# A fixed TensorE order for the RWKV preparation: one stretch of small products per pair, head sums in shared banks

## The chip, the cores and the metric

The kernel runs on one core of a Trainium2 chip. The metric is the device time of one execution in microseconds (us). TensorE multiplies matrices out of SBUF into the eight banks of PSUM; VectorE (DVE) and ScalarE (ACT) read those banks and compute elementwise; GpSimd (POOL) works on SBUF alone; transfers are issued from the queues of SyncE (SP), ScalarE and GpSimd. The engines run side by side and wait for each other through semaphores.

## What is computed

One decoder layer on 512 tokens of width 1024, in float32. Attention sub-layer: a norm, one wide input projection, and two mixers on its columns, a sparse attention (compressed, selected and window branches) and an RWKV-7 mixer with 8 heads of 64; both are projected, merged by gates, projected again and added. Channel sub-layer: norm, a gated MLP with a short causal convolution, add. The change lies in the preparation of the RWKV mixer, of which this is the core:

```python
xl = p_in + (shifted - p_in) * mu
r, k, v, xw, xa, xg = jnp.split(xl, RWKV_SPLITS, axis=-1)
w = -jax.nn.softplus(-(w0 + jnp.tanh(xw) @ w2)) - 0.5
decay = jnp.exp(-jnp.exp(w.astype(jnp.float32)))
a = jax.nn.sigmoid(a0 + xa @ a2)
...
kk = k * k_k.reshape(H, N).astype(jnp.float32)
kk = kk / jnp.maximum(jnp.sqrt(jnp.sum(kk * kk, axis=-1, keepdims=True)), 1e-12)
k = k * (1.0 + (a - 1.0) * k_a.reshape(H, N).astype(jnp.float32))
...
y = y + jnp.sum(r * k * r_k, axis=-1, keepdims=True) * v
```

Two sums over the 64 channels of a head stand in it: the norm of `kk` (key sum) and the bonus `sum(r * k * r_k)`.

## The kernel before

Activations lie with channels on the 128 partitions and the 512 tokens along the row; two heads share a tile, so the 8 heads make four pairs p = 0 to 3 (`NH2`). To keep float32 accuracy every large product is made of three: weights and activations are split into a high and a low part (`whi`, `wlo`; `hh`, `hl`), and a dense tile of 128 columns (`dense_fm`, line 414) is 8 steps of `whi` times `hh` and `whi` times `hl`, then 8 of `wlo` times `hh`: 24 products of 128x128 by 512. Each dense tile takes the next weight tile from a fixed list (`weight_tiles`, line 215): `wnext` starts the load of a later tile on SP, splits the one after (`wsplit_`: high part on ScalarE, low part on VectorE or GpSimd, line 296) and hands out the one in turn.

For a pair the preparation has these steps. `front(p)` (492): the dense tile of keys, the two decay products `zw` and `za` (64 rows each, on the two halves of the array), token shift (`shift_mix`: one ScalarE and one VectorE operation out of the bank), tanh, a cumulative sum by a VectorE scan, two exponentials `ep` and `pi`. `norms(p)` (516): squares of the scaled keys (`kk`), the key sum as one product of the block matrix `ones` with `kk`, maximum, logarithm, exponential, giving `rn`. `receptance(p)` and `values_of(p)`: the dense tiles of `rx` and `vx`. `values_tok(p)` (538): four transposes of `vx` into one bank and four ScalarE copies into `UV`. `vectors(p)` (548): some ten VectorE operations from these to `AR`, `bh` and `tv`, then the bonus sum as one product of `ones` with `tv`, times `vx`, into `BO`. `gram(p)` (567): 16 transposes of `bh` into two banks, copied to `BKT` by ScalarE; then 32 products of `bh` with `AR` in two halves of four chunks, each into two banks, masked by VectorE into `AB`.

PSUM banks come from three rings: `mmb()` with four banks, `pa()` and `pb()` with two each. A product that starts a bank waits until the last reader of that bank's previous content is done.

The order of the instructions on each engine is chosen when the program is built, from the order in the text, the dependencies and estimated durations; `tc.high_priority()` moves an instruction ahead. Inside `tc.manual_schedule(engines=...)` the named engines follow the text instead. The preparation is outside such a block before the change, so the small products of one step may stand between the dense products of another.

Behind the preparation, VectorE inverts the 32x32 diagonal blocks of `AB` (lines 617 to 633: four transposes, 62 small operations), transposes the result into `Y1` (730), and `below` (740) multiplies with it on TensorE. In between TensorE makes dense tiles of queries, compressed values and the first key and value windows. The queries' read-out (688 to 692) copies each bank and squares each head into a part of `QK` that serves as scratch. At 696 to 704 the bias table is expanded: a memset on GpSimd, two small loads on ScalarE's queue into the same part of `QK`, one product, one copy, one store.

## Time and profile before

| | us |
|---|---|
| median of 3 runs | 841.3 |
| lowest and highest | 841.02, 841.45 |
| the profiled execution | 841.33 |
| its span in the profile | 839.5 |

The profile is one execution. A row of the list in order of time gives the start from the beginning of the span, the length, the engine, the line, the operation, what it writes and reads, and the shape; several alike are merged into one row with their count, and the idle time of the engine before it, with what ended it, stands in brackets. Almost all operations go through small helpers, so that line 120 is every product, 123 every ScalarE operation, 126 to 135 most of VectorE's: names of tiles tell them apart. A float32 product appears as two instructions, one for each of two passes. Matmuls are pipelined: what counts is the distance from one start to the next, not the length shown. PE is TensorE, ps_mm, ps_a and ps_b are the three rings of banks, kc holds the constants (`ones`, the identity, the mask), prm the parameters.

### The profile page before, as it was taken

How to read it: one execution, taken by the hardware profiler on the slowest of the kernel's cores; microseconds unless marked ns; L12 is line 12 of the kernel's file. 1: busy time of each engine (PE TensorE's matmuls, PEld its weight loads, DVE VectorE, ACT ScalarE, POOL GpSimd, SP SyncE). 2: the span in 40 equal slices, each digit the busy share in tenths (PEclk: the TensorE clock that was granted, in tenths of full speed). 3: DMA queues.
4: the chain of work that ended last, by engine and by line, in shares of the span. 5: the costliest groups of instructions: out<-in, count | busy, mean ns of one | idle time of the engine just before them, and what ended most of it. 6: DMA issues, size and time to landing. Idle time of an engine off the chain costs nothing.

```text
span 839.5 us, 12845 instructions
## 1 busy us (share of the span) xinstructions
PE 824.8 (98%) x5097; PEld 669.9 (80%) x5097; DVE 514.1 (61%) x998; ACT 405.4 (48%) x784; POOL 52.4 (6%) x69
## 2 busy tenths in 40 slices
PE   7999999999999999999999999999999999999998
PEld 6777778887677876777788988888888888888886
DVE  5478779964556678888665566665555666322222
ACT  6766654452555767677343454444444444221210
POOL 5200020140000100111000000000000000000000
PEclk9999999999999999999999999999999999999999
DMA  7432222335462320000266033333333332233421
GB/s 229 113 80 72 76 76 77 83 102 168 128 126 62 84 57 13 26 26 26 63 222 206 1 101 100 94 90 93 101 101 101 100 96 89 92 101 113 138 75 51
DMA packets 109104, 78.73 MB, mean 94 GB/s; under 512 B 3869, under 2 KB 97748, under 8 KB 109044
## 3 DMA queue, kind: packets, MB, share of 16 engines
q1 hardware_dynamic: 106512, 73.51, 29.7%
q10 hardware_dynamic: 1060, 2.55, 1.0%
q0 software_dynamic: 1472, 1.86, 1.0%
q8 instruction: 40, 0.66, 0.3%
q14 instruction: 20, 0.16, 0.1%
HBM read 74.56 MB, written 2.29 MB: 92 GB/s over the span
## 4 chain that ended last, share of the span: by engine, by line
PE 53%; DVE 0%; DVEq 0%; issue 0%
PE ps_mm L120 52%; PE ps_b L203 0%; PE ps_a L203 0%; PE ps_a L120 0%; PE ps_b L1187 0%; PE ps_mm L1187 0%; DVE x L126 0%; DVEq L1379 0%; PE ps_a L1139 0%
## 5 line engine op out<-in xcount | busy, mean ns | idle before, releaser
L296 DVE TENSOR_TENSOR wlo<-raw,whi 128x1024 fp32r<-128x1024 f32 (+1 forms) x111 | 131.5, 1186 | 186.5 <-PE ps_mm L120 157.8
L120 PE MATMUL ps_mm<-hh,whi 128*128 128x512 f32 (+1 forms) x624 | 242.6, 391 | 0.7 <-ACT whi L123 0.7
L120 PE MATMUL ps_mm<-hl,whi 128*128 128x512 f32 (+1 forms) x624 | 240.4, 387 | 0.0
L123 ACT ACTIVATE whi<-raw 128x1024 fp32r<-128x1024 f32 (+3 forms) x124 | 123.3, 996 | 170.9 <-PE ps_mm L120 141.6
L120 PE MATMUL ps_mm<-hh,wlo 128*128 128x512 f32 (+1 forms) x624 | 151.7, 384 | 0.0
L120 PEld LDWEIGHTS ps_mm<-hh,whi 128*128 128x128 f32 x624 | 117.3, 188 | 27.5 <-ACT whi L123 1.1
L120 PEld LDWEIGHTS ps_mm<-hl,whi 128*128 128x128 f32 x624 | 117.4, 188 | 23.4 <-issue 1.0
L120 PEld LDWEIGHTS ps_mm<-hh,wlo 128*128 128x128 f32 x624 | 115.1, 188 | 23.3
L120 PE MATMUL ps_mm<-whi,aT 128*128 128x512 f32 x352 | 84.5, 390 | 0.0
L120 PEld LDWEIGHTS ps_mm<-whi,aT 128*128 128x128 f32 x352 | 65.9, 188 | 14.3 <-issue 0.4
L135 DVE SCALAR_TENSOR_TENSOR cgv<-ps_mm,cw,cgv 128x511 f32<-128x511 f32 (+1 forms) x88 | 65.4, 746 | 1.6
L123 ACT ACTIVATE cgv<-ps_mm,cw 128x512 f32<-128x512 f32 x44 | 34.3, 781 | 23.3 <-PE ps_mm L120 23.3
L120 PE MATMUL ps_mm<-wlo,aT 128*128 128x512 f32 x176 | 44.3, 389 | 0.0
L123 ACT ACTIVATE P<-P,nm 128x512 f32<-128x512 f32 (+3 forms) x64 | 35.4, 553 | 14.9 <-DVE nm L1161 14.9
L123 ACT ACTIVATE aT<-cgv 128x512 fp32r<-128x512 f32 x22 | 13.9, 632 | 56.8 <-DVE cgv L126 56.8
L120 PEld LDWEIGHTS ps_mm<-wlo,aT 128*128 128x128 f32 x176 | 33.0, 188 | 6.9
L123 ACT ACTIVATE cgv<-cgv 128x512 f32<-128x512 f32 x22 | 13.9, 632 | 41.0 <-DVE cgv L135 41.0
L296 POOL TENSOR_TENSOR wlo<-raw,whi 128x512 fp32r<-128x512 f32 (+3 forms) x13 | 20.4, 1569 | 204.3 <-PE ps_mm L120 148.5
L1161 DVE CUSTOM_DVE_ANT_0 P<-ps_a,AB 128x512 f32<-128x512 f32 (+3 forms) x64 | 29.4, 483 | 4.2 <-PE ps_a L120 3.7
L126 DVE TENSOR_TENSOR x<-x,ps_mm 128x512 f32<-128x512 f32 (+1 forms) x17 | 11.0, 654 | 23.0 <-PE ps_mm L120 21.2
L126 DVE TENSOR_TENSOR aT<-cgv,aT 128x512 fp32r<-128x512 f32 x22 | 15.2, 693 | 14.7 <-ACT aT L123 14.7
L120 PE MATMUL ps_a<-KH,qst 128*128 128x512 f32 (+3 forms) x64 | 21.3, 348 | 1.6 <-DVE nm L1161 0.9
(356 smaller groups left out, 1203.4 us busy)
## 6 DMA issues: line engine op xcount, KB each, us to landing
raw<-in_w_up_dram SPq DMA_DIRECT2D x44, 512.0 KB, 3.7
raw<-in_w_in_dram SPq DMA_DIRECT2D x38, 512.0 KB, 3.8
raw<-in_w_down_dram SPq DMA_DIRECT2D x22, 512.0 KB, 3.5
raw<-in_w_out_dram SPq DMA_DIRECT2D x8, 512.0 KB, 3.6
xt<-in_x_dram SPq DMA_DIRECT2D x4, 512.0 KB, 5.9
raw<-in_cmp_w_k_dram SPq DMA_DIRECT2D x4, 512.0 KB, 4.9
raw<-in_cmp_w_v_dram SPq DMA_DIRECT2D x4, 512.0 KB, 5.0
raw<-in_w_proj_b_dram SPq DMA_DIRECT2D x8, 256.0 KB, 2.7
```

Of the source, the lines that this page charges most:

```text
L120: te.matmul(o, lhsT=l, rhs=r, start=start, stop=stop)
L123: sc.activation(o, i, f, **kw)
L126: v.tensor_tensor(o, a, b, op=op)
L135: v.scalar_tensor_tensor(o, a, s, b, op0=op0, op1=op1)
L296: eng.tensor_tensor(lo, raw, hi.bitcast(F32), op=ALU.subtract)
L1161: v.tensor_tensor_reduce(out=P[:, i], in0=sp[:, N * (i - i0):N * (i - i0) + N], in1=BT[:, h, 384 - 128 * qt:512], scale=-1.0, scalar=-NEG, ...
```

## The change

- `front` and the sum in `norms` are taken apart: `keys_of` (dense keys, shift, squares), `decays` (decay products and what follows), `norms` (what follows the sum).
- A head sum is no longer one product of 128x128 by 512. `head_sums` makes four of 64x64 by 256: the first 256 tokens go to bank 0 with the two heads in place, the second 256 to bank 1 with the two heads exchanged, so that the four lie on the four quarters of the array. The readers undo the exchange in pieces (`EXCH`). `sums` puts the key sum of the next pair in columns 0 to 255 and the bonus sum of this pair in columns 256 to 511 of the same two banks.
- `kk` is overwritten with the clipped sum; the maximum is two operations, the last exponential three, the multiplication with `vx` three, each on half or a quarter of the data.
- TensorE's order is written out: vector work of the pair, dense keys and receptance of the next pair, then in one stretch the value transposes, the next pair's decay products, `gram`, the shared sums, and the next pair's dense values. For the last pair but one, decay products lie inside the receptance tile (after 12 of its 24 products) and the key sum right behind it, ahead of the value transposes.
- `gram` takes its transposes' banks and, by pair, one half's banks from `mmb` instead; the copies to `BKT` have priority.
- After the preparation, the squares of the queries are written in place into their bank, and the bias table's memset and two loads come ahead of the queries, the loads on GpSimd's queue.

```diff
--- before.py
+++ after.py
@@ -489,14 +489,18 @@
     L = {}
 
 
-    def front(p):
+    def keys_of(p):
+        kx = t2("kx", 2)
+        shift_mix(dense_fm(hh, hl), 4 + p, kx)
+        kk = t2("kk", 2)
+        act(kk, kx, AF.Square, scale=col("rwkv_k_k", p))
+        L.setdefault(p, {}).update(kx=kx, kk=kk)
+
+    def decays(p):
         cs = slice(128 * p, 128 * p + 128)
-        kx = t2("kx", 2)
-        pk = dense_fm(hh, hl)
         zw, za = pa(), pb()
         mm(zw, wa[0:64, cs], xw[0:64], True, True)
         mm(za, wa[64:128, cs], xw[64:128], True, True)
-        shift_mix(pk, 4 + p, kx)
         cl = t2("cl")
         act(cl, zw, AF.Tanh, scale=0.5, bias=w0h[:, p:p + 1])
         aa = t2("aa", 2)
@@ -511,23 +515,32 @@
         pi = t2("pi", 2)
         act(pi, cum, AF.Exp, scale=-1.0)
         v.tensor_copy(PC[:, p, :, None], ep[:, :, C:C + 1])
-        L[p] = dict(kx=kx, aa=aa, ep=ep, pi=pi)
-
-    def norms(p):
-        kx = L[p]["kx"]
-        kk = t2("kk", 2)
-        act(kk, kx, AF.Square, scale=col("rwkv_k_k", p))
-        ss = pa()
-        mm(ss, ones, kk, True, True)
+        L.setdefault(p, {}).update(aa=aa, ep=ep, pi=pi)
+
+
+
+    def head_sums(src, o, o0=0):
+        for i in range(2):
+            for r in range(2):
+                a, b = slice(64 * r, 64 * r + 64), slice(64 * (r ^ i), 64 * (r ^ i) + 64)
+                mm(o[i][b, o0:o0 + 256], ones[a, a], src[a, 256 * i:256 * i + 256], True, True)
+
+    EXCH = [(slice(0, 128), slice(0, 128), 0), (slice(0, 64), slice(64, 128), 1), (slice(64, 128), slice(0, 64), 1)]
+
+    def norms(p, o):
+        kk = L[p]["kk"]
         rn = t2("rn", 2)
-        ts(rn, ss, 1e-24, None, op0=ALU.max)
-        act(rn, rn, AF.Ln)
-        act(rn, rn, AF.Exp, scale=-0.5)
-        L[p].update(kk=kk, rn=rn)
+        for i in range(2):
+            ts(kk[:, 256 * i:256 * i + 256], o[i][:, 0:256], 1e-24, None, op0=ALU.max)
+        act(kk, kk, AF.Ln)
+        for d, s_, i in EXCH:
+            cs = slice(256 * i, 256 * i + 256)
+            act(rn[d, cs], kk[s_, cs], AF.Exp, scale=-0.5)
+        L[p]["rn"] = rn
 
     def receptance(p):
         rx = t2("rx", 2)
-        shift_mix(dense_fm(hh, hl), p, rx)
+        shift_mix((yield from dense_fm_g(hh, hl)), p, rx)
         L[p]["rx"] = rx
 
     def values_of(p):
@@ -559,23 +572,38 @@
         stt(bh[:, :, 1, :], chunks(kx), 1.0, chunks(pi), ALU.mult, ALU.mult)
         tv = t2("tv")
         stt(tv, rx, col("rwkv_r_k", p), kx, ALU.mult, ALU.mult)
-        L[p]["bh"] = bh
-        bs = pa()
-        mm(bs, ones, tv, True, True)
-        tt(BO[:, p], bs, vx, ALU.mult)
+        L[p].update(bh=bh, tv=tv)
+
+    def bonus(p, o):
+        for d, s_, i in EXCH:
+            cs = slice(256 * i, 256 * i + 256)
+            tt(BO[d, p, cs], o[i][s_, 256:512], L[p]["vx"][d, cs], ALU.mult)
+
+
+    def sums(pk, pb_):
+        o = [pa(), pb()]
+        if pk is not None:
+            head_sums(L[pk]["kk"], o)
+        if pb_ is not None:
+            head_sums(L[pb_]["tv"], o, 256)
+        if pk is not None:
+            norms(pk, o)
+        if pb_ is not None:
+            bonus(pb_, o)
 
     def gram(p):
         bh = L[p]["bh"]
-        ptr = [pb(), pa()]
+        ptr = [mmb(), mmb()]
         for c in range(NCH):
             for r in range(2):
                 rs = slice(64 * r, 64 * r + 64)
                 te.transpose(ptr[r][:, 64 * c:64 * c + 64], bh[rs, c, r:r + 2].rearrange("p a t -> p (a t)"),
                              ident[rs, rs])
-        for r in range(2):
-            act(BKT[:, :, p, r, :], ptr[r].rearrange("p (c j) -> p c j", c=NCH))
+        with tc.high_priority():
+            for r in range(2):
+                act(BKT[:, :, p, r, :], ptr[r].rearrange("p (c j) -> p c j", c=NCH))
         for c0 in range(0, NCH, 4):
-            ptr = [mmb(), mmb()] if c0 else [pb(), pa()]
+            ptr = [mmb(), mmb()] if c0 == (0, 0, 4, -1)[p] else [pb(), pa()]
             for i in range(4):
                 for r in range(2):
                     rs = slice(64 * r, 64 * r + 64)
@@ -586,24 +614,34 @@
                    mask[:, None, :].to_broadcast([128, 4, 128]), ALU.mult)
 
 
-    front(0)
-    norms(0)
-    receptance(0)
-    values_of(0)
-    late_params()
-    for p in range(NH2):
-        if p + 1 < NH2:
-            front(p + 1)
-            norms(p + 1)
-        values_tok(p)
-        vectors(p)
-        if p + 1 < NH2:
-            receptance(p + 1)
-        gram(p)
-        if p + 1 < NH2:
-            values_of(p + 1)
-        if p + 2 == NH2:
-            kcp = dense_fm(hh, hl)
+    with tc.manual_schedule(engines={mybir.EngineType.PE}):
+        keys_of(0)
+        decays(0)
+        run(receptance(0))
+        sums(0, None)
+        values_of(0)
+        late_params()
+        for p in range(NH2):
+            vectors(p)
+            last = p + 2 == NH2
+            if p + 1 < NH2:
+                keys_of(p + 1)
+                rec = receptance(p + 1)
+                next(rec)
+                if last:
+                    decays(p + 1)
+                run(rec)
+                if last:
+                    sums(p + 1, None)
+            values_tok(p)
+            if p + 1 < NH2 and not last:
+                decays(p + 1)
+            gram(p)
+            sums(p + 1 if p + 1 < NH2 and not last else None, p)
+            if p + 1 < NH2:
+                values_of(p + 1)
+            if p + 2 == NH2:
+                kcp = dense_fm(hh, hl)
     dbg("AR", AR)
     dbg("BO", BO)
     close(tp_cm)
@@ -682,21 +720,21 @@
             for r in range(2):
                 act(Dc[64 * r:64 * r + 64, a, g, :], p[64 * g:64 * g + 64, r::2])
 
+    oh, rbx, vb = QK[0:33, 2048:2432], QK[0:33, 2440:2448], QK[0:8, 2560:2944]
+    nc.gpsimd.memset(rbx[32:33], NEG)
+    nc.gpsimd.dma_start(rbx[0:32], A["rel_bias"])
+    nc.gpsimd.dma_start(oh, A["onehot"])
     windows(0, kcp)
     urgent.append(1)
     bq = dense_tok(512, hh, hl)
     for t in range(NT):
         act(qn[:, t], bq[t])
         for h in range(H):
-            act(QK[:, 2048 + 64 * h:2112 + 64 * h], bq[t][:, 64 * h:64 * h + 64], AF.Square,
-                accum_out=qss[:, t, h:h + 1])
+            hs_ = bq[t][:, 64 * h:64 * h + 64]
+            act(hs_, hs_, AF.Square, accum_out=qss[:, t, h:h + 1])
     windows(1, dense_fm(hh, hl))
 
 
-    oh, rbx, vb = QK[0:33, 2048:2432], QK[0:33, 2440:2448], QK[0:8, 2560:2944]
-    nc.gpsimd.memset(rbx[32:33], NEG)
-    sc.dma_start(rbx[0:32], A["rel_bias"])
-    sc.dma_start(oh, A["onehot"])
     pt = pa()
     mm(pt[0:8, 0:384], rbx, oh, True, True)
     act(vb, pt[0:8, 0:384])
```

## The prediction

> **What bounds the kernel now.** I read the page first, then the sums by stretch, then the preparation in order of time on TensorE, and last what ScalarE and VectorE do under it.
>
> ```profile
> span 839.5 us, 12845 instructions
> PE 824.8 (98%) x5097; PEld 669.9 (80%) x5097; DVE 514.1 (61%) x998; ACT 405.4 (48%) x784; POOL 52.4 (6%) x69
> ```
>
> TensorE has 98% of the span and nothing else comes near it. The change touches 31.54 us (first decay product) to 123.03 us (first query product):
>
> ```profile
> 31.54:123.03 91.49, 90.96 (x532) 68.89 (x531) 67.67 (x103) 57.94 (x84) 2.35 (x1) 1.00 0.26 72
> 51.02:73.49 22.47, 22.47 (x133) 17.17 (x133) 17.11 (x27) 14.48 (x21) 0.00 (x0) 1.00 0.18 48
> L120 PE MATMUL ps_mm<-hh,wlo 128*128 128x512 f32 x97 | 24.1, 389 | 0.0
> 29.64 1.98 PE L120 MATMUL ps_mm<-hh,wlo 128*128 128x512 f32 x8
> ```
>
> In the first two rows the numbers after the length are busy time and count of TensorE, its weight loads, VectorE, ScalarE and GpSimd. TensorE is busy 90.96 of 91.49 us at a full granted clock (1.00), VectorE 67.67, ScalarE 57.94, the DMAs 0.26 of their time. The third row counts the low-part products: 97, one begun earlier, so 96, a third of 288 dense products (12 weight tiles of 24). The fourth gives their pitch, (1.98 - 0.389) / 7 = 0.227 us. Dense work is 288 x 0.2265 = 65.2 us, and 91.5 - 65.2 = 26.3 us is everything else on TensorE. In one pair (22.47 us, 72 dense products of 16.3 us) it is 6.2 us. That is what the change can shrink.
>
> **What the small work costs now.** Pair 0 to 1, in order of time, with start and length first:
>
> ```profile
> 50.70 0.39 PE L120 MATMUL ps_mm<-hh,wlo 128*128 128x512 f32 x1
> 51.02 0.69 PE L120 MATMUL ps_a<-xw,wa 64*128 64x512 f32 x1
> 52.08 0.66 PE L542 MATMUL ps_b<-kc,vx 128*128 128x128 f32 x4
> 52.49 0.48 PE L120 MATMUL ps_mm<-hh,whi 128*128 128x512 f32 x1
> 52.81 0.39 PE L120 MATMUL ps_mm<-hl,whi 128*128 128x512 f32 x1
> 54.65 1.02 PE L120 MATMUL ps_a<-kk,kc 128*128 128x512 f32 x2
> 55.52 1.02 PE L120 MATMUL ps_a<-tv,kc 128*128 128x512 f32 x2
> 59.91 0.27 PE L573 MATMUL ps_b<-kc,bh 64*128 64x64 f32 x1
> 60.45 0.33 PE L120 MATMUL ps_b<-AR,bh 64*128 64x128 f32 x1
> 62.39 0.50 PE L120 MATMUL ps_mm<-hh,whi 128*128 128x512 f32 x1
> ```
>
> From start to start: decay pair 51.02 to 52.08, 1.06; value transposes 0.41; a head sum (kk, then tv) 0.87; key transposes 59.91 to 60.45, 0.54; gram products 60.45 to 62.39, 1.94. Leaving a dense run costs 50.70 to 51.02, 0.32 instead of 0.23; returning, 52.49 to 52.81, the same: 0.2 us for a stretch in all. Over four pairs: 4.2 + 1.65 + 7.0 (eight sums) + 2.15 + 7.75, with 0.35 for the parameter transposes, is 23.1. There are 13 stretches (two in the first pair's lead, one for parameters, three for each of three pairs, one at the end): 2.6. The rest, about 0.6 to 0.9, is waiting, most of it at the end:
>
> ```profile
> 118.76 0.66 PE L542 MATMUL ps_b<-kc,vx 128*128 128x128 f32 x4 [0.25 <-DVE vx L135]
> 120.69 0.22 PE L573 MATMUL ps_a<-kc,bh 64*128 64x64 f32 x1
> 121.05 0.37 PE L120 MATMUL ps_b<-AR,bh 64*128 64x128 f32 x1
> 124.18 0.50 PE L120 MATMUL ps_mm<-whi,hh 128*128 128x512 f32 x1 [0.18 <-DVE AB L126]
> ```
>
> **The head sums.** Each becomes four products of 64 rows by 64 columns on four quarters of the array, 256 columns long, two to a bank. No row shows that form at 256. The nearest is the scan:
>
> ```profile
> 187.26 0.27 PE L120 MATMUL ps_b<-Xs,AB 64*64 64x64 f32 x2
> 187.28 0.27 PE L120 MATMUL ps_b<-UV,AB 64*64 64x64 f32 x2
> 187.37 0.23 PE L120 MATMUL ps_b<-Xs,AB 64*64 64x64 f32 x2
> ```
>
> Four quarter products start within 0.02 us and the next four follow 0.1 us later, so quarters run side by side, with the two of one output bank in different partitions. Half the columns of the 0.87 us sum then take 0.43. Bounds: 0.43, or 0.87 if they run in twos. I take 0.43: 8 x 0.44 = 3.5 us gained. [...]
>
> **The order.** Stretches fall from 13 to 8: decay 0, sum 0, parameters, pair 0, pair 1, decay 3, pair 2, pair 3. 5 x 0.2 = 1.0 us gained. Inside a merged stretch the tile shape changes twice; a first product costs 0.33 against 0.27 (60.45 and 59.91 against their followers), about 0.05 each, 0.4 us lost in all. The old waits go (0.9). Sum before new waits: 3.5 + 1.0 - 0.4 + 0.9 = **5.0 us**.
>
> **New waits.** A fixed order cannot slip dense work in while a bank is read out. In pairs 0 and 1 the shared sums need both banks of the decay products, and each of those is released by ScalarE, which in the same stretch has:
>
> ```profile
> L123 ACT ACTIVATE UV<-ps_b 64x256 f32<-64x256 f32 x4 | 1.5, 378 | 0.1
> L123 ACT ACTIVATE cl<-ps_a,w0h 128x512 f32<-128x512 f32 x1 | 0.7, 690 | 0.4 <-PE ps_b L120 0.4
> L123 ACT ACTIVATE rx<-ps_mm,omm 128x512 f32<-128x512 f32 x1 | 0.7, 687 | 0.0
> L123 ACT ACTIVATE aa<-ps_b,a0h 128x512 f32<-128x512 f32 x1 | 0.7, 681 | 0.0
> L123 ACT ACTIVATE BKT<-ps_a 128x512 f32<-128x512 f32 x1 | 0.6, 600 | 0.0
> L123 ACT ACT_TABLE_LOAD x2 | 2.6, 1283 | 0.0
> ```
>
> 1.5 + 0.7 + 0.7 + 0.7 + 2 x 0.6 = 4.8 us, some 4.6 with their overlap. TensorE reaches the sums after 0.41 + 1.06 + 0.54 + 1.94 + 0.1 = 4.05. So about 0.6 us of waiting twice, 1.2; queued behind the sums are only the value products. In pair 2 the bonus sum waits likewise, 0.3 estimated (up to 3, if the logarithm's two table loads of 1.28 go ahead of the transposes' read-out). In pair 3 the second gram half needs the bank of the value transposes; that cost 0.36 before (120.69 to 121.05), and the key copies (2 x 0.6) now have priority over it: 0.6 taken, 0.4 to 1.4 possible. New waits: 1.2 + 0.3 + 0.6 = **2.1 us**, bounds 0 and 5.6.
>
> **What is hidden.** The norm's logarithm and exponential and the bonus come in two and three pieces. A 64-partition, 256-column copy out of PSUM takes 0.43 on VectorE:
>
> ```profile
> L957 DVE COPY UV<-ps_b x8: 427/428/428, 188.9 to 279.7; 64x256 f32<-64x256 f32 x8
> 55.71 0.69 DVE L130 TENSOR_SCALAR rn<-ps_a 128x512 f32<-128x512 f32 x1 [0.19 <-PE ps_a L120]
> 71.21 0.74 DVE L135 SCALAR_TENSOR_TENSOR tv<-rx,prm,kx 128x512 f32<-128x512 f32 x1
> 82.38 0.27 PE L573 MATMUL ps_b<-kc,bh 64*128 64x64 f32 x1
> ```
>
> So three pieces of bonus are 1.3 instead of 0.7 and two of the maximum 0.86 instead of 0.69: +0.8 us of VectorE a pair, 17.9 in some 21.5. The chain from a key sum to the next gram (maximum, logarithm, exponential, eight vector operations) ran from 55.71 to 71.21, 15.5 us, and had until 82.38. Now three dense tiles (16.3) and 1.5 of small work lie between: 17.8. The cover shrinks from 26.7 to 17.8 but holds by 2.3. Price 0; without that cover see the rival below.
>
> After the stage, VectorE runs a long inverse which TensorE meets at `below`:
>
> ```profile
> 124.64 8.16 DVE L625 STREAM_TRANSPOSE inv<-AB 32x1024 f32<-32x1024 f32 x4
> 163.24 4.46 DVE L730 STREAM_TRANSPOSE sg<-inv 32x1024 f32<-32x1024 f32 x2
> 168.94 0.21 PE L120 MATMUL ps_a<-sg,AB 32*32 32x32 f32 x1
> ```
>
> It ends at 167.70, 1.24 us before it is needed. The last bonus (1.3) now stands between masks and transposes, while TensorE has the last sum (0.43 + 0.2) there too: about 0.5 us of slack is left, price 0, bound 0.8.
>
> The moved loads leave ScalarE's queue, where the weight split followed them, for GpSimd's:
>
> ```profile
> 149.14 0.33 ACTq L698 DMA_DIRECT2D QK<-in_rel_bias_dram  x1
> 20.15 0.56 POOL L437 DMA_DIRECT2D wa<-in_rwkv_w_dram  x1 [0.92 <-PE ps_mm L120]
> 124.36 2.40 POOL L296 TENSOR_TENSOR spare<-raw,spare 128x1024 fp32r<-128x1024 f32 x1
> ```
>
> Two issues of 0.33 go from ScalarE; two of 0.56 on GpSimd may delay the spare split, which dense queries use only some 8 us after its end. The squares change only where they write. Price 0, between -0.3 and +0.3.
>
> **Sum.** The profiled execution took 841.33 us, 1.83 around its span of 839.5; the median of the runs, 841.3, is the same. 841.33 - 5.0 + 2.1 = **838.4 us**.
>
> **Rivals.**
> - No new waits: ScalarE keeps ahead as it has 8 of 22.47 us free in a pair. 841.3 - 5.0 = 836.3. Against: its work in the stretch, 4.6, does not fit 4.05.
> - The waits eat the gain, so the merged stretch does not do what it is said to: bounds of 5.6 against 5.0 give 841.9. For: the table loads sit in the same engine. Against: ScalarE is idle elsewhere, so banks can be read before.
> - The quarters do not overlap in one bank: 3.5 lost, 838.4 + 3.5 = 841.9. [...]
> - Slower: the chain to the next gram is late. Its place is VectorE's queue right after the shared sums, where masks (4 x 0.6), bonus (1.3), scale and scan (1.6) now stand ahead of or among the norm: 15.5 + 5.3 = 20.8 against 17.8, 3 us at each of pairs 1, 2 and 3, 838.4 + 9 = 847. It decides from a total of 4.6 us late, since 838.4 + 4.6 = 843.0. Against: in the old 15.5 us four masks and a bonus are already included.
>
> **How the numbers follow.** About 0.2% (1.7 us) is what a measurement of this kernel can tell from no change. Forecast 0.52, no waits 0.16: both faster, 0.68. Waits eat the gain 0.13, quarters 0.05: same, 0.18. Late chain 0.14: slower. The range goes from 835.8 (5.0 gained without a wait, 0.3 from the moved loads, 0.2 more) to 842.5, which holds the two rivals near 841.9 and leaves most of the late chain outside. The forecast's own range is 836.3 to 839.9.
>
> **What would show it.** Right: no kk or tv product of 512 columns; eight stretches; quarter products of a sum starting within 0.02 us, a shared pair of sums in about 0.9 us; a pair's period near 21.4; waits of TensorE on `cl` or `aa` of about 0.6 before the sums. Wrong: a wait on `bh` before the key transposes, a period above 22.5, sums of 1.7 us, or `below` waiting for the inverse.

## The result, and the profile after

The changed kernel takes 844.99 us (median of 6 runs, 844.34 to 845.53) against 841.33 for the kernel before on the same chip: ratio 1.0043, 95% interval 1.0032 to 1.0054. It is 3.7 us slower, where 2.9 us faster was predicted. The page of the profile after:

```profile
span 843.2 us, 12971 instructions
PE 825.1 (98%) x5145; PEld 671.2 (80%) x5145; DVE 516.5 (61%) x1010; ACT 409.2 (49%) x792; POOL 53.3 (6%) x71
```

The span grew by 3.7 us, TensorE's busy time by 0.3. So the time went into TensorE's idle time, except for what a slower clock adds. The sums by stretch, for the preparation and for its pair periods (columns as in the prediction; the granted clock stands behind the five busy times):

```profile
31.45:127.44 95.99, 91.54 (x580) 70.48 (x580) 69.99 (x114) 60.31 (x92) 2.35 (x1) 0.98 0.25 67
55.81:78.05 22.24, 22.24 (x145) 17.62 (x144) 17.06 (x30) 13.42 (x21) 0.00 (x0) 1.00 0.28 71
78.05:103.97 25.92, 23.87 (x149) 17.74 (x148) 18.43 (x30) 15.76 (x25) 0.00 (x0) 1.00 0.25 63
103.97:123.28 19.31, 17.12 (x116) 13.42 (x117) 16.10 (x26) 13.51 (x21) 0.00 (x0) 0.91 0.26 76
...
109.00:112.20 3.20, 3.20 (x31) 2.22 (x27) 2.74 (x5) 3.15 (x6) 0.00 (x0) 0.50 0.42 152
```

The preparation takes 95.99 us, 4.5 more than 91.49. The period of pair 0 to 1, 22.24, is 0.2 shorter than before and has no idle time. In the next one TensorE is idle for 25.92 - 23.87 = 2.05 us, in the third for 2.19, and there its clock falls to half for one stretch of 3.4 us, which costs 1.7. The places, in order of time on TensorE:

```profile
59.98 0.65 PE L120 MATMUL ps_a<-kk,kc 64*64 64x256 f32 x4
60.58 0.43 PE L120 MATMUL ps_b<-kk,kc 64*64 64x256 f32 x2
...
82.47 1.04 PE L120 MATMUL ps_mm<-AR,bh 64*128 64x128 f32 x13 [2.00 <-DVE rx L135]
...
105.12 0.66 PE L555 MATMUL ps_b<-kc,vx 128*128 128x128 f32 x4 [0.49 <-ACT aa L123]
...
108.12 0.37 PE L120 MATMUL ps_b<-AR,bh 64*128 64x128 f32 x1 [1.70 <-DVE kk L130]
...
109.28 1.92 PE L120 MATMUL ps_mm<-AR,bh 64*128 64x128 f32 x16
```

The first two rows show the wait that was predicted: the second bank of the sums is held by `aa`, and its products start at 60.58 instead of within 0.1 of 59.98. It makes the two sums about 0.5 longer: 1.61 here and 1.51 in the next pair, against 1.08 in run 7 below, which does not wait for `aa`. The large waits are others. The gram of pair 1 waits 2.00 for a bank of the ring of four until VectorE has done the shift of `rx`; that of pair 2 waits 1.70 for the bank of the key sum until VectorE has taken its maximum. The last row is the half clock: 16 starts in 1.85 us, where at full clock they take 0.99. Of the 4.5 us lost, 0.9 comes back behind the preparation: `below` starts 4.50 later than before (173.44, 168.94), the last state product of the scan 3.63 later (273.32, 269.69), since in between the kernel before waits 0.69 for the split of a weight that has just landed (212.36) and the changed kernel does not.

Why is VectorE late? ScalarE and VectorE of the kernel after, from one norm to the waiting gram, in order of time:

```profile
64.32 0.42 DVE L130 TENSOR_SCALAR kk<-ps_b 128x256 f32<-128x256 f32 x1
64.82 1.28 ACT L123 ACT_TABLE_LOAD   x1 [2.94 <-DVE kk L130]
...
68.06 1.27 ACT L123 ACTIVATE rn<-kk 128x256 f32<-128x256 f32 x3
69.37 0.75 DVE L135 SCALAR_TENSOR_TENSOR kk<-kx,prm,rn 128x512 f32<-128x512 f32 x1 [3.73 <-ACT rn L123]
...
78.05 0.75 DVE L135 SCALAR_TENSOR_TENSOR kx<-ps_mm,prm,kx 128x511 f32<-128x511 f32 x1
78.83 0.72 ACT L123 ACTIVATE kk<-kx,prm 128x512 f32<-128x512 f32 x1 [5.33 <-DVE kx L135]
81.67 0.74 DVE L135 SCALAR_TENSOR_TENSOR rx<-ps_mm,prm,rx 128x511 f32<-128x511 f32 x1
```

VectorE waits 3.73 us for the exponential `rn`. From 69.37 to 78.05 it is busy without a break (vector work of pair 1, the shift of `vx`, two weight splits), and only then comes the shift of pair 2's `kx`, on which ScalarE has waited for 5.33 us, and behind it, with one split more, that of `rx`. Whatever makes `rn` late makes these shifts late. From this norm to the next one (93.74) neither engine waits for TensorE: VectorE works until 78.80, ScalarE from 78.83 to 83.35 (squares, a weight split, `rx`, `UV`, `cl`), VectorE from 83.38 to 89.12 (scan, masks, maximum, bonus), ScalarE from 89.19 to 93.70 (logarithm, exponentials, two table loads). These 24.37 us are a loop of the two engines alone, and TensorE's waits follow from it. The experiments took that apart.

### The profile page after: what moved, and what is told of

Its sections match the earlier page's. It is cut to its first block, busy times and chain, and to the rows that moved or that the text cites. A ratio compares the mean times of both kernels' runs of the same rounds, so it can differ in the third digit from the quotient of the medians.

```text
span 843.2 us, 12971 instructions
## 1 busy us (share of the span) xinstructions
PE 825.1 (98%) x5145; PEld 671.2 (80%) x5145; DVE 516.5 (61%) x1010; ACT 409.2 (49%) x792; POOL 53.3 (6%) x71
## 4 chain that ended last, share of the span: by engine, by line
PE 53%; DVE 0%; DVEq 0%; issue 0%
PE ps_mm L120 52%; PE ps_a L203 0%; PE ps_b L203 0%; PE ps_a L120 0%; PE ps_b L1225 0%; PE ps_mm L1225 0%; DVE x L126 0%; DVEq L1417 0%; PE ps_a L1177 0%
## 5 line engine op out<-in xcount | busy, mean ns | idle before, releaser
L120 PE MATMUL ps_mm<-whi,hh 128*128 128x280 f32 (+2 forms) x72 | 22.6, 334 | 0.3 <-ACT QK L123 0.3
```

Of the source, the lines that this page charges most:

```text
L120: te.matmul(o, lhsT=l, rhs=r, start=start, stop=stop)
```

## The experiments

Times are medians; each ratio is to the kernel before, run in turn on the same chip. The rows and waits are those of one profiled execution of each. The diffs show the deciding lines, and `...` stands for the others.

**1. The moved loads and squares alone** (the kernel before with these two edits).

```diff
-            act(QK[:, 2048 + 64 * h:2112 + 64 * h], bq[t][:, 64 * h:64 * h + 64], AF.Square,
...
+            act(hs_, hs_, AF.Square, accum_out=qss[:, t, h:h + 1])
...
-    sc.dma_start(rbx[0:32], A["rel_bias"])
+    nc.gpsimd.dma_start(rbx[0:32], A["rel_bias"])
...
```

> The kernel before with only the last part of the change: squares in place, the bias table's two loads ahead of the queries on GpSimd's queue. Theory W (the loss is bank waits of the fixed order: 2.2 us on rx in pair 1, 0.6 + 1.9 on aa and kk in pair 2, 1.6 of half clock behind it): this part weighs nothing, 841.0 to 841.6. Rival L (the moved loads cost): 842.5 or more, with a longer stretch between the first query product and the inverse's first use than 45.9 us.

841.39 us, ratio 0.9998 (0.9989 to 1.0008). This part weighs nothing.

**2. The quarter sums alone** (the kernel before, its own order; sums and readers as changed, one bank of `pa` and one of `pb` for each sum).

```diff
-        ss = pa()
-        mm(ss, ones, kk, True, True)
+        o = [pa(), pb()]
+        head_sums(kk, o)
...
```

> The kernel before, order left free, with each head sum as four quarter products of 256 columns in two banks and its readers in pieces. Theory W: the sums gain, 8 x (0.87 - 0.52) = 2.8 us less the extra tile shapes (8 x 0.1): 839.0 to 840.0. Rival Q (quarter products and shape changes cost what they save): 841.0 or more.

848.62 us, ratio 1.0078 (1.0065 to 1.0092): alone it is worse than the whole change. TensorE waits at the first gram product of three pairs; one of them:

```profile
87.26 0.37 PE L120 MATMUL ps_b<-AR,bh 64*128 64x128 f32 x1 [1.44 <-ACT UV L123]
```

The bank is that of the value transposes, whose four copies `UV` ScalarE spreads between the norm's table loads. The sums' second bank has pushed them closer together in a ring of two.

**3. The changed kernel without the written order** (the block of manual order removed).

```diff
-    with tc.manual_schedule(engines={mybir.EngineType.PE}):
+    if True:
```

> The changed kernel with the written order of TensorE taken off its preparation, all else kept. Theory W: dense products fill the waits on rx, aa and kk again, no half clock, 839 to 842. Rival Q or L: it stays at 844 to 846.

844.81 us, ratio 1.0037 (1.0025 to 1.0050). The order that results has the same stretches and waits (1.99 for `rx`, 1.70 for `kk`), so the block as such is not the cause. Whether dense work slipped into the waits would help is not shown, as none was.

**4. Vector work behind the next keys.**

```diff
-            vectors(p)
             last = p + 2 == NH2
             if p + 1 < NH2:
                 keys_of(p + 1)
+            vectors(p)
+            if p + 1 < NH2:
```

> The changed kernel with the vector operations of a pair written behind the next pair's keys instead of ahead of them; TensorE's order is the same. Theory W, with VectorE's burst as the cause of the late read-out: the keys' shift is no longer 5 us late, squares and weight split come earlier, rx is read at once, the wait of 2.2 us in pair 1 goes, pair 2 partly: 841.5 to 843. Rival (the banks' assignment alone decides, not the burst): within 0.5 us of 845.0.

845.03 us, ratio 1.0039 (1.0026 to 1.0052). VectorE's order hardly changed by it: the shift of `kx` starts at 78.20 and the wait for `rx` stays at 1.99. The run tells nothing about the cause, but the half clock now came behind this wait, at 83.84, instead of at 108.9.

**5. Quarter sums, with the value transposes' bank taken from the ring of four.**

```diff
-        pt = pb()
+        pt = mmb()
```

> The kernel before with every head sum as four quarter products (as in the run that took 848.6), but the bank of the value transposes is taken from the ring of four (mm) instead of the ring of two (b) whose other user is now the second bank of each sum. Theory (bank turnover): the three waits of 1.5 to 1.6 us at the first gram product, each for ScalarE's UV copies, go away, and what the shorter sums give (8 x (0.87 - 0.55) = 2.6) is seen: 839 to 842. Rival (the quarter products and their changes of tile shape are dear by themselves): nothing changes at the sums, 846 or more.

842.72 us, ratio 1.0017 (1.0008 to 1.0025), 5.9 less than run 2: the shared ring was that run's loss. What remains are three waits of 0.7 to 1.8 for the shift of `vx` on VectorE. The profiled execution also has 6.8 us at half clock behind the last one; but it took 844.64, while eight of the eleven took 842.5 to 843.1 with a granted clock of 0.998 or more.

**6. The order alone: whole sums, key sum in the first bank, bonus sum in the second.**

```diff
-            head_sums(L[pk]["kk"], o)
+            mm(o[0], ones, L[pk]["kk"], True, True)
-            head_sums(L[pb_]["tv"], o, 256)
+            mm(o[1], ones, L[pb_]["tv"], True, True)
...
```

> The changed kernel's order with each head sum as one product of 512 columns again (key sum in the first bank, bonus sum in the second). Theory (bank turnover): the order has the same banks and the same readers, so its waits of 0.45 to 2.2 us stay, and the eight sums are 0.35 longer each: 846.5 to 848.5, slower than the change as it is. Rival (quarters and shape changes are dear): without them below 843.

841.51 us, ratio 1.0002 (0.9993 to 1.0011). The theory held until then, that crowding the small products into one stretch keeps them waiting for banks, fell here: the same order with the same rings of banks has one wait of 0.74 (for `vx`, in the last pair) and none else above 0.2, no half clock, and a preparation of 91.43 us. ScalarE and VectorE of this run at the place shown above:

```profile
61.30 0.61 ACT L123 ACTIVATE pi<-cum 128x512 f32<-128x512 f32 x1
61.93 1.28 ACT L123 ACT_TABLE_LOAD   x1
...
63.70 0.68 DVE L130 TENSOR_SCALAR rn<-ps_a 128x512 f32<-128x512 f32 x1
64.41 0.63 ACT L123 ACTIVATE rn<-rn 128x512 f32<-128x512 f32 x1 [1.20 <-DVE rn L130]
...
66.36 0.63 ACT L123 ACTIVATE rn<-rn 128x512 f32<-128x512 f32 x1
67.02 0.75 DVE L135 SCALAR_TENSOR_TENSOR kk<-kx,prm,rn 128x512 f32<-128x512 f32 x1 [2.05 <-ACT rn L123]
...
75.71 0.74 DVE L135 SCALAR_TENSOR_TENSOR kx<-ps_mm,prm,kx 128x511 f32<-128x511 f32 x1
```

Everything is 2.35 us earlier from the norm on (67.02 against 69.37). Three things make the difference. The logarithm's table load starts right behind `pi`, ahead of its data; in the changed kernel it starts only behind the second half of the maximum, so its 1.28 lies on the chain. One exponential takes 0.63 instead of 1.27 for three. The maximum ends at 64.38 instead of 64.74. Sum: 1.28 + 0.64 + 0.36 = 2.28.

**7. The changed kernel with every pair's decays in the middle of the receptance.**

```diff
-                if last:
-                    decays(p + 1)
+                decays(p + 1)
...
```

> The changed kernel with the next pair's decay products in the middle of the receptance for every pair (the change does so for the last one only). Theory (bank turnover, with each wait set by its own reader): the sums no longer wait for aa (0.45 twice), the gram's waits for rx and kk stay as their readers are not touched: two stretches more cost 0.4, so 844 to 845.3. Rival (the waits come from the mere amount of ScalarE's work within the stretch): cl and aa (1.4 us of ScalarE) leave the stretch and the waits for rx and kk fall by as much in two pairs: 842.5 or less.

843.53 us, ratio 1.0025 (1.0014 to 1.0035), 1.5 less than the change and a little below the expected 844 to 845.3. The preparation shrank from 95.99 to 94.36: the sums no longer wait for `aa`, and the half clock did not occur. The gram's waits did not go: 1.17, 1.52 and 0.67 in the three pairs (none, 2.00 and 1.70 in the changed kernel), with a new one of 0.85 behind the third.

A further variant, the gram a dense tile later so that `rx` and `kk` are read before, needs a second buffer for `vx`; that takes 51.6 KB a partition where 50 KB are left, so it has no time.

The next four take the chain of the norm apart.

**8. Whole sums, but read in pieces.**

```diff
-        ts(rn, o, 1e-24, None, op0=ALU.max)
-        act(rn, rn, AF.Ln)
-        act(rn, rn, AF.Exp, scale=-0.5)
+        for i in range(2):
+            ts(kk[:, 256 * i:256 * i + 256], o[:, 256 * i:256 * i + 256], 1e-24, None, op0=ALU.max)
+        act(kk, kk, AF.Ln)
+        for d, i in PIECES:
...
+            act(rn[d, cs], kk[d, cs], AF.Exp, scale=-0.5)
...
```

> The changed kernel's order with each head sum as one product of 512 columns (that took 841.5), but read out in pieces as the change does it: maximum in two halves, logarithm on the whole, exponential in three pieces, bonus in three. Theory (the pieces make the norm's chain late: the exponential is done at 69.33 instead of 66.99, as the table load for the logarithm now starts only behind the maximum, 1.28, three exponentials take 1.27 instead of 0.63, and the maximum ends 0.4 later; VectorE's queue then holds up the shifts of kx and rx, whose banks the gram needs): the waits of 2.0 and 1.7 and the half clock of the changed kernel come back, 841.5 + 5.3 = 846.8, 845 to 848.5. Rival (the quarter products themselves cost it): the products are whole here, so it stays at 841.5, below 843.

843.87 us, ratio 1.0036 (1.0022 to 1.0050). The pieces alone cost 2.4 us on the order alone, without a single quarter product. Expected were 5.3 with a half clock in them; the profiled execution has none, and the one execution of six with a granted clock of 0.995 took 846.87. VectorE gets `rn` 1.79 later than in run 6, and TensorE waits:

```profile
68.81 0.75 DVE L135 SCALAR_TENSOR_TENSOR kk<-kx,prm,rn 128x512 f32<-128x512 f32 x1 [3.41 <-ACT rn L123]
...
82.02 1.04 PE L120 MATMUL ps_mm<-AR,bh 64*128 64x128 f32 x13 [1.55 <-DVE rx L135]
```

**9. The changed kernel with the logarithm's table loaded early**, by a logarithm of one column of `pi` whose result is not used.

```diff
+    lnw = cp.tile([128, 1], F32, name="lnw")
...
+        act(lnw, L[p]["pi"][:, 0:1], AF.Ln)
         act(kk, kk, AF.Ln)
```

> The changed kernel with a logarithm of one column of pi right behind the exponential that makes pi, whose result nobody reads: its table load is done while the sums run, and the norm's logarithm needs none. Theory (late chain): 1.28 off the chain, so the gram's waits of 2.0 and 1.7 fall by about 1.3 each, and with pauses below a us the half clock (1.6) goes: 845.0 - 1.3 - 1.3 - 1.6 = 840.8; 842.4 if the half clock stays. Rival (quarter products): 845.

850.40 us, ratio 1.0111 (1.0098 to 1.0124): a miss, most of it not in the preparation. There `rn` comes 1.41 earlier, the wait for `rx` falls from 2.00 to 0.65, and no half clock is seen; but in the last pair a wait of 1.62 for `bh` is new (run 18), so that the preparation still takes 94.56. The loss of 7 us lies in the up projections, 350 us later (runs 14 and 18).

**10. The changed kernel with a short chain**: the exchange of the halves in the maximum, ahead of the bonus; logarithm and exponential whole.

```diff
+        with tc.high_priority():
+            for d, s_, i in EXCH:
...
+                ts(rn[d, cs], o[i][s_, 0:256], 1e-24, None, op0=ALU.max)
+        act(rn, rn, AF.Ln)
+        act(rn, rn, AF.Exp, scale=-0.5)
```

> The changed kernel with the exchange of the halves moved from the exponential to the maximum: three maxima ahead of the bonus, then logarithm and exponential on the whole tile. Theory (late chain): the exponential is 0.63 instead of 1.27, the maximum ends 0.1 to 0.2 later, so 0.5 off each of the gram's waits of 2.0 and 1.7: 844.0, and 842.4 if the half clock goes with it; if the table load is taken early again, as it was with the maximum in one piece, 1.28 more in each pair, 840. Rival (quarter products): 845.

842.13 us, ratio 1.0016 (1.0006 to 1.0025), 2.9 less than the change. The table load is early again without help, and the wait for `rx` is down to 0.54:

```profile
61.89 1.28 ACT L123 ACT_TABLE_LOAD   x1
65.30 0.63 ACT L123 ACTIVATE rn<-rn 128x512 f32<-128x512 f32 x1 [2.13 <-DVE rn L130]
...
81.01 1.04 PE L120 MATMUL ps_mm<-AR,bh 64*128 64x128 f32 x13 [0.54 <-DVE rx L135]
```

**11. Both edits of 9 and 10.**

```diff
...
+        act(lnw, L[p]["pi"][:, 0:1], AF.Ln)
         act(rn, rn, AF.Ln)
```

> Both: the exchange in the maximum and the logarithm of one column ahead of it. Theory (late chain): 1.8 off the chain, which takes it to within 0.6 of the whole sums' (that waited for nothing above 0.6), so the gram's waits and the half clock go: 845.0 - 1.8 - 1.7 - 1.6 = 839.9, 838.5 to 841, faster than before. Rival (quarter products): 845.

849.06 us, ratio 1.0096 (1.0083 to 1.0110). In the preparation it is run 10 (wait for `rx` 0.55), with the loss of run 9 behind it.

**12. The kernel before with quarter sums, their own ring, and the short chain** (the edits of 2, 5 and 10).

```diff
-        ss = pa()
+        o = [pa(), pb()]
...
+                ts(rn[d, cs], o[i][s_, 0:256], 1e-24, None, op0=ALU.max)
...
-        pt = pb()
+        pt = mmb()
...
```

> The kernel before in its own order, each head sum as four quarter products, value transposes in the ring of four (that took 842.7), and the exchange of the halves in the maximum, ahead of the bonus, so that logarithm and exponential are whole. Theory (the quarters gain a little, 0.15 to 0.3 a sum, and what undoes it is the norm's chain through VectorE's queue): the waits for vx (0.8, 0.7, 1.8) shrink by 0.4 to 0.5 each, and the half clock behind the last of them (2.9) goes: 842.7 - 1.4 - 2.9 = 838.4; 841.3 if the half clock stays. Faster than before in the first case. Rival (quarter products give nothing in either order): 841.4 or more.

840.57 us, ratio 0.9986 (0.9977 to 0.9995), the fastest of all, but not the 838.4 expected. The first and the last of its three periods, and VectorE's norm of pairs 2 and 3 with the transposes that wait:

```profile
50.95:72.91 21.96, 21.96 (x146) 16.86 (x145) 17.71 (x30) 14.49 (x21) 0.00 (x0) 1.00 0.21 53
...
94.86:118.80 23.94, 22.10 (x146) 16.86 (x145) 19.70 (x31) 14.61 (x21) 1.38 (x1) 1.00 0.24 66
```

```profile
85.77 0.74 DVE L135 SCALAR_TENSOR_TENSOR kk<-kx,prm,rn 128x512 f32<-128x512 f32 x1
108.25 0.74 DVE L135 SCALAR_TENSOR_TENSOR kk<-kx,prm,rn 128x512 f32<-128x512 f32 x1
...
118.80 0.66 PE L553 MATMUL ps_mm<-kc,vx 128*128 128x128 f32 x4 [1.52 <-DVE vx L135]
```

TensorE's period falls from 22.47 to 21.96: two sums as quarters are 0.51 shorter. But VectorE goes from norm to norm in 108.25 - 85.77 = 22.48 us, within 0.03 us of the times of the kernel before:

```profile
85.74 0.74 DVE L135 SCALAR_TENSOR_TENSOR kk<-kx,prm,rn 128x512 f32<-128x512 f32 x1
...
98.39 1.22 DVE L506 TENSOR_TENSOR_SCAN cum<-scanm,cl 128x512 f32<-128x512 f32 x1
99.65 0.63 ACT L123 ACTIVATE ep<-cum 128x512 f32<-128x512 f32 x1 [0.25 <-DVE cum L506]
...
106.83 0.69 ACT L123 ACTIVATE rx<-ps_mm,omm 128x512 f32<-128x512 f32 x1
107.55 0.75 DVE L135 SCALAR_TENSOR_TENSOR rx<-ps_mm,prm,rx 128x511 f32<-128x511 f32 x1 [1.31 <-ACT rx L123]
108.22 0.74 DVE L135 SCALAR_TENSOR_TENSOR kk<-kx,prm,rn 128x512 f32<-128x512 f32 x1
```

These rows close a loop without TensorE: VectorE is busy without a break from the norm to the end of the scan (99.61), ScalarE from there to the end of `rx` (107.52), with both table loads in between, and VectorE's shift of `rx` and the next norm follow at once.

So TensorE gains a lead of 1.1 us in two periods and in the third waits 1.52 for VectorE. The quarters shorten TensorE's period, and the loop through VectorE and ScalarE, as long as that period was, takes it back. The 0.8 us by which this run is faster are not shown to be theirs: its preparation is 0.2 longer than before (91.69 against 91.49). In the profiled execution (840.92) the gain lies behind it, where a weight's split starts 0.48 earlier (210.77 against 211.25, both behind its transfer) and the wait of 0.69 at 212.36 is gone.

**13. Run 10 with the decays apart.**

```diff
-                if last:
-                    decays(p + 1)
+                decays(p + 1)
...
```

> The changed kernel with the exchange in the maximum (842.1) and the next pair's decays in the middle of the receptance in every pair. Theory: the sums no longer wait for aa (0.45 in two pairs), two stretches more cost 0.3 together: 842.1 - 0.9 + 0.3 = 841.5, 840.5 to 842. It does not beat the kernel before by more than can be measured, as the pair before last still waits 1.4 for the maximum. Rival (fewer banks in the stretch free ScalarE for rx and UV too): 840 or less.

841.11 us, ratio 0.9995 (0.9987 to 1.0004): as expected, no difference from the kernel before.

**14. Run 9 with an unused tile of 64 instead of 4 bytes a partition.**

```diff
-    lnw = cp.tile([128, 1], F32, name="lnw")
+    lnw = cp.tile([128, 16], F32, name="lnw")
...
```

> The changed kernel with the early logarithm of one column once more (that took 850.4), its unused tile now 16 columns (64 bytes a partition) wide instead of one (4 bytes). Theory (the 7 us that the early logarithm lost lie in the up projections, far behind the preparation, where a dense product's pitch was 0.233 instead of 0.2265; everything allocated behind the new tile stood 4 bytes further on): with 64 bytes the pitch is 0.2265 again, and what is left is the gain of the shorter chain, 850.4 - 7.0 = 843.4. Rival (the early logarithm itself does it, by the tables or the clock): 850.

849.98 us, ratio 1.0104 (1.0090 to 1.0118). The guess of an offset of 4 bytes fell.

**15 to 17. Twelve weight splits on GpSimd**, in the kernel before (control), in run 12's kernel and in the changed one.

```diff
-                yield cols(w_in, O_RWKV + o + 128 * p)
+                yield cols(w_in, O_RWKV + o + 128 * p, eng=pool_)
```

> Control: the kernel before with the low half of the preparation's twelve weight tiles (keys, receptance, values of four pairs) subtracted by GpSimd instead of VectorE, 12 x 1.22 us less on VectorE. Theory (in the kernel before VectorE's chain just fits under TensorE: its waits for VectorE in the preparation are 0.2 to 0.4): at most 0.5 gained, 840.8 to 841.6. Rival (the split by GpSimd, 2.40 as in the spare split, comes too late for the low products): slower, 843 or more.

> The run of 840.6 (own order, quarter sums, short chain) with the same twelve subtractions on GpSimd. Theory (the quarters gain 0.25 a sum, and in the last period it is lost again as TensorE waits 1.5 for vx behind VectorE's queue, which ran at the very times of the kernel before): without 1.22 three times a period VectorE is no longer late, 840.6 - 1.5 = 839.1, 838.3 to 839.9, faster than both kernels. Rival (VectorE is not what binds): 840.6 as without it.

> The changed kernel, nothing undone, with the same twelve subtractions on GpSimd. Theory (its waits are those of VectorE's queue: the gram's bank waits for rx and kk, whose shifts and maxima stand behind the norm's late vector operations and two of these subtractions): the wait of 2.0 for rx goes, that of 1.7 for kk falls by 1.2, no half clock: 845.0 - 2.0 - 1.2 - 1.6 = 840.2, 839 to 842. Rival (quarter products, or banks that ScalarE releases): 844 to 845.

843.36 us (ratio 1.0021, 1.0012 to 1.0030), 841.88 (1.0002, 0.9993 to 1.0011) and 850.95 (1.0111, 1.0097 to 1.0125): each slower than without the move. The edit did not do what it was meant to. GpSimd and VectorE of the third run:

```profile
72.45 5.40 POOL L296 TENSOR_TENSOR wlo<-raw,whi 128x1024 fp32r<-128x1024 f32 x2 [11.96 <-ACT whi L123]
```

```profile
72.83 2.77 DVE L135 SCALAR_TENSOR_TENSOR kk<-aa,kk 128x512 f32<-128x512 f32 x1
```

This vector operation on SBUF and another at 75.64 (`bh<-kk,pi`), which take 0.69 otherwise, last about as long as GpSimd's two subtractions (2.7 each): 2.77. VectorE saved three splits of 1.22 a period and lost more. As a test of the theory the third run still counts, in the other direction: its VectorE goes from norm to norm in 26.51 us instead of 24.37, and the wait for `rx` grows from 2.00 to 2.58.

**18. Run 9 without a new tile**: the unused logarithm is written into `rn`, which is overwritten later.

```diff
+        act(rn[:, 0:1], L[p]["pi"][:, 0:1], AF.Ln)
         act(kk, kk, AF.Ln)
```

> The changed kernel with the early logarithm of one column written into rn, which the norm overwrites later, so that no tile is added. Theory (the 7 us lost in the up projections belong to the place of the tiles in memory, which one more tile moves): the pitch there is 0.2265 again and the gain of the shorter chain is left, 845.0 - 1.5 = 843.5, 842 to 844. Rival (the early logarithm itself does it): 850.

844.10 us, ratio 1.0034 (1.0021 to 1.0047). The 7 us are gone, so they belonged to the added tile and not to the logarithm. Of the chain's gain 1.6 is lost again in the last pair: beside a split on GpSimd (119.51 to 121.86) one vector operation for `bh` takes 2.28 instead of 0.69, and the key transposes wait 1.6 for it.

## Why the prediction was wrong

VectorE's distance from one norm (`kk<-kx,prm,rn`) to the next, from pair 1's to pair 2's, beside TensorE's wait at the gram of pair 1 (for `rx`, in runs 7 and 13 for `BKT`):

| kernel | norm to norm | wait at the gram | preparation | time |
|---|---|---|---|---|
| order alone, whole sums (6) | 22.33 | none | 91.43 | 841.5 |
| before | 22.48 | none | 91.49 | 841.3 |
| quarters, short chain, old order (12) | 22.49 | none | 91.69 | 840.6 |
| short chain, decays apart (13) | 22.78 | 0.42 | 91.71 | 841.1 |
| short chain (10) | 22.93 | 0.54 | 92.76 | 842.1 |
| decays apart (7) | 23.86 | 1.52 | 94.36 | 843.5 |
| whole sums in pieces (8) | 24.03 | 1.55 | 94.47 | 843.9 |
| changed | 24.37 | 2.00 | 95.99 | 845.0 |
| changed, order free (3) | 24.37 | 1.99 | 96.01 | 844.8 |
| changed, vectors later (4) | 24.37 | 1.99 | 95.37 | 845.0 |
| changed, splits on GpSimd (17) | 26.51 | 2.58 | 102.19 | 851.0 |

In these kernels the preparation grows with the first column, with quarters or with whole sums. The column is one period of three, and several of the runs left out lose time in other places too: run 2 at `UV` (24.35, 97.90), run 5 at half clock (22.73, 95.35), runs 9, 14 and 18 in the last pair (23.0, 94.6 to 95.6).

- *The step that failed* is "What is hidden", the price 0 for the norm's pieces. It counted 0.8 us of VectorE's work and took the chain to the gram as covered by 2.3. The runs show three things in its place. The chain grew by 2.35 on ScalarE and VectorE together (run 6), most of it a table load of 1.28 that run 6 does before its data are there, and three exponentials for one. The cover was measured for `bh` alone; but the shifts of the next `kx` and `rx` stand in VectorE's queue behind the same vector operations, and they had no cover, as the bank of `rx` is asked for by the gram right behind the receptance. And the pieces cost 2.4 us without any quarter product (run 8).
- *What bounds the kernel*: TensorE's 98% was read as "nothing else comes near". VectorE at 67.67 of 91.49 us is not busy all the time, but with its waits for ScalarE it forms a loop of 22.48 a pair, equal to TensorE's 22.47. That the two are equal would say little by itself, as engines that wait for each other share a period; but no wait for TensorE lies on the loop, and it stayed when TensorE's period fell to 21.96 (run 12). A gain on TensorE alone had nowhere to go.
- *The head sums*: that the quarters overlap was right, and it took away the rival that doubted it. The size was wrong: 0.44 a sum was taken, 0.25 each was measured for two together (run 12), and 0.08 for one alone. The rows of the changed kernel and of run 6, at the first sum:

```profile
37.64 0.61 PE L120 MATMUL ps_mm<-hh,wlo 128*128 128x512 f32 x2
38.19 0.43 PE L120 MATMUL ps_a<-kk,kc 64*64 64x256 f32 x2
38.20 0.43 PE L120 MATMUL ps_b<-kk,kc 64*64 64x256 f32 x2
38.46 0.38 PE L120 MATMUL ps_a<-kk,kc 64*64 64x256 f32 x2
...
38.78 0.50 PE L120 MATMUL ps_mm<-hh,whi 128*128 128x512 f32 x1
39.12 0.39 PE L120 MATMUL ps_mm<-hl,whi 128*128 128x512 f32 x1
```

```profile
37.37 0.85 PE L120 MATMUL ps_mm<-hh,wlo 128*128 128x512 f32 x3
38.06 1.02 PE L120 MATMUL ps_a<-kk,kc 128*128 128x512 f32 x2
38.52 0.80 PE L120 MATMUL ps_mm<-hh,whi 128*128 128x512 f32 x1
39.15 0.40 PE L120 MATMUL ps_mm<-hl,whi 128*128 128x512 f32 x1
```

From the last dense product (37.87; 37.82 in run 6) to the second one behind the sum it is 1.25 with quarters and 1.33 with the whole sum. A first pass of 256 columns takes 0.27 (38.19 to 38.46). The changes of shape show in the steps around: 0.1 going in (0.32 instead of 0.23) and 0.2 coming out (0.31 and 0.34 for two steps of 0.23). The whole sum, of the dense shape, goes in with a step of 0.24 (37.82 to 38.06). In the prediction only 0.05 for a change of shape inside a stretch was set aside. The four products start within 0.02 us (38.19 and 38.20), two to a bank in different partitions.
- *The order*: eight stretches came as predicted. Its own sum (1.5 gained without the quarters, 2.1 of waits) said 0.6 slower; run 6 says 0.2 slower with an interval from 0.6 faster to 0.9 slower. That they agree is in part luck. TensorE's work in the stretches fell by 0.49 in run 6 (busy 90.47 of 91.43 instead of 90.96 of 91.49), where 0.6 was taken. But the 0.9 of old waits that were to go was too much: TensorE's idle time before was 91.49 - 90.96 = 0.53, and one of the two waits shown (124.18) lies behind the end at 123.03. In run 6 it is 0.96, so the new waits were too large as well. In the changed kernel the waits for `aa` came as predicted, about 0.5 instead of 0.6. A pair's period, forecast as 21.4, is 22.24 (22.35 in run 6).
- *The late chain* was among the rivals, with 0.14 and 847: the right place (VectorE's queue behind the shared sums). That 847 lies near 845.0 is luck: it sets 9 us of waits on a gain of 2.9, while the runs show waits of 2.00 and 1.70 and almost no gain. And its sign was a wait on `bh`, and in the changed kernel `bh` is in time; the wait appears a step later, at the gram's banks.
- *The half clock* was in no term. It makes up 1.7 of the 4.5 us in the profiled execution. What the change would take without it is open: one of its six executions has a granted clock of 1.000, and that one took 844.76.
- *Price 0 for the inverse and the loads* was right: `below` starts 46.00 behind the first query product, 45.91 before, and run 1 is even.

## What to carry to other kernels

Before an engine at 98% is taken as the bound, measure the loop of each other engine from one operation to the same operation of the next stage. Here it equalled the bound's own period (22.48 and 22.47 us) and held no wait for the bound: a gain of 0.51 a pair on the bound alone was taken back (run 12), and 2.4 us of pieces added to the loop showed (run 8). When an edit cuts a reader into pieces, follow the whole queue behind it, the operations that merely stand behind it too, up to the bank they hold. And look at whether a table load runs ahead of its data or behind it: an edit that adds no arithmetic, the maximum in two halves, moved its 1.28 us onto the path here.

## What the hardware showed beyond that

- *Vector operations were longer beside a GpSimd subtraction.* `kk<-aa,kk` and `bh<-kk,pi` took 2.77 (run 17) and `bh<-kx,pi` 2.28 (run 18), each 0.69 without one.
- *The clock fell to half behind some short pauses.* In the changed kernel the drop at 108.9 follows a stretch in which TensorE worked half of the time:

```profile
105.50:108.90 3.40, 1.70 (x33) 1.40 (x32) 3.37 (x7) 3.12 (x7) 0.00 (x0) 1.00 0.17 20
```

It lasted 3.4 us; in run 4 it followed the wait of 1.99, in run 5 one of 1.77. In run 8, with a wait of 1.55, and in the changed kernel behind the wait of 2.00 it did not come. It differs between executions of one kernel, too: five of the changed kernel's six have a granted clock of 0.997 or 0.998, one has 1.000. What decides stays open.
- *With a tile added elsewhere, dense products came 2.8% more slowly.* With one unused tile in the pool of constants (run 9, then run 18 without it):

```profile
520.00:560.00 40.00, 40.00 (x173) 32.18 (x173) 23.36 (x29) 16.99 (x21) 0.00 (x0) 1.00 0.33 95
```

```profile
520.00:560.00 40.00, 40.00 (x178) 33.10 (x178) 23.79 (x30) 18.15 (x23) 0.00 (x0) 1.00 0.36 105
```

In 40 us of the up projections TensorE begins 173 products instead of 178, at a full granted clock and without a wait. With 4 and with 64 bytes it is 173 (runs 9 and 14). What of the tile decides was not tried.
- *Where the logarithm's table load stands* changed with the way the maximum was written: behind it with two halves into `kk` (64.82, the second half from 64.32), ahead of it with one operation into `rn` (61.93 and 63.70 in run 6) or three (61.89 in run 10). Why was not tried.
